# A hybrid encoder block on one core: the head of the u projection with joined loads, a second load of the first token block, filler products on a constant, and gate stores issued by SyncE

## The chip, the cores and the metric

The kernel runs on one core of one Trainium2 chip. The metric is the device time of one execution in microseconds, taken as the median of several runs.

## The reference

All data are float32. The block is one layer of the following, on 1040 rows (16 meta rows and 1024 tokens) of 1024 channels.

```python
def _mixer(xn, w_in, b_forget, ...):
    proj = xn @ w_in                                    # 1024 -> q, k, v, f_logit, u, gates
    q, k, v, f_logit, u, gates = jnp.split(proj, SPLITS, axis=-1)
    y_a = _forgetting_attention(q, k, v, f_logit, b_forget) @ w_attn_out
    z = jax.nn.gelu(_s5(u, ...))                        # diagonal complex state space model
    zg = z @ w_glu
    y_s = zg[..., :D_MODEL] * jax.nn.sigmoid(zg[..., D_MODEL:])
    g = jax.nn.sigmoid(gates)
    return (g[..., :D_MODEL] * y_a + g[..., D_MODEL:] * y_s) @ w_o

def reference(x, meta_tokens, ...):
    h = jnp.concatenate([meta, x], axis=1)
    h = h + _mixer(_rmsnorm(h, norm_mix_g), ...)
    h = h + _conv_ffn(_rmsnorm(h, norm_ffn_g), ...)     # causal depthwise conv, width 3
    return _rmsnorm(h, norm_final_g)[:, N_META:]
```

Here `u` is 512 channels wide, `gates` 2048, and `_s5` sends `u` in 32 groups of 16 channels through 64 complex states each.

## The kernel before, in words

**Products.** Every matrix product is a sum of three matmuls. An operand is split into a rounded part (`xhi`, `uh`, `whi`) and the remainder (`xlo`, `ul`, `wlo`), and hi·hi, lo·hi and hi·lo are added up in PSUM. The rounding is a cast on ACT, the remainder a subtraction on DVE or, for gate weights, an accumulating DMA (L144).

**The head.** The first product is `u`, the projection that feeds the state space model. The tokens lie transposed (channels on partitions, 8 chunks of 128, `KD = 8`) in four blocks of 272, 256, 256 and 256 tokens (`UBLK`). Block 0 is worked on while it is still being loaded: `FIRST` lists how many of the eight chunks come with each pair of loads, one load of `xa` (tokens) and one of `uraw` (the rows of the weight of u). For each chunk `features` makes `xhi` (ACT, L383) and `xlo` (DVE, L384), the weight is cast to `uh` (ACT, L409) and `ul` (DVE, L137), and `part` issues the products for the four groups of 128 channels of u (PE, L351 to L353) into four PSUM banks held open over all chunks. The loads are issued by SyncE (SP) in a fixed order through `load` (L313). They go on with blocks 1 to 3 (`xT`) and the tokens again with tokens on partitions (`xt`, `xm`), from which the root mean squares are taken.

**The normed features.** The u products use the tokens times the gain `g1T` alone, since the factor 1/rms of a token can be applied to the product. The gate and attention products need it in their input. So, once block 3 has been multiplied, `factors(b)` and `normed_features(b)` build the factors, multiply the raw blocks that are still in SBUF by them and split the result anew into `xhi` and `xlo`, block after block.

**Stores of u.** The u product goes through `usb` to DRAM (`u_d`) in 32 stores, 16 issued by SP and 16 by POOL (L455), and comes back in another layout as `U` (L1910): the first two of these loads are issued by SP.

**Gates.** `gate_chunk` multiplies one chunk of 128 gate channels, in three pieces of 342 rows, takes the sigmoid on ACT (L505) and stores the piece to DRAM (`g_d`), the store being issued by POOL (L506). The very first chunk has tiles of its own, `g0s`. All later pieces share two buffers of `gs`, so a sigmoid writes into a buffer whose store before last must have landed. The weights of each chunk are loaded by POOL (`raw`, L148) and cast by ACT (`whi`, L154).

**State space model.** Between the gate products the steps of the state space model run. For one quarter of the groups: DVE makes `Vm`, PE transposes it (L1903), ACT copies the result to `Wi` (L1904), PE multiplies `U` by `Wi` (L1916), ACT copies the products to `wr` and `wi` (L1919 and L1920), DVE does the recurrence on them (L1639 and two scans), and the same for the next quarter. `Tm` is loaded from `Kt` by SP (L1889).

**Order.** A scheduler settles the order of the instructions on each engine when the program is built. Each engine works through its list in that order, and one that waits holds up all that stands behind it.

Of the kernel before, what the change touches and what calls it, by code (L numbers as in the profile page):

```python
# [9 lines left out]
F = mybir.dt.float32  # L10
# [9 lines left out]
P = 128  # L20
D = 1024
KD = D // P
META = 16
# [5 lines left out]
SW = 512  # L29
# [14 lines left out]
UBLK = [(0, 272), (272, 256), (528, 256), (784, 256)]  # L44
UN = UBLK[0][1]
# [10 lines left out]


@with_exitstack
def block_kernel(ctx, tc, x, meta, xbt, x0t, g1t, w_q, w_k, w_v, w_f, w_u, w_g, b_f, w_ao, lam_d, bw_d, cw_d,
                 d_sk, l_dt, w_glu, w_o, g2, w_up, cwt_d, w_dn, gf, out, dbg=None, upto=99):  # L60
    nc = tc.nc
    dbg = dbg or {}
# [2 lines left out]
    V, S, GP, PE, SY = nc.vector, nc.scalar, nc.gpsimd, nc.tensor, nc.sync  # L65
# [7 lines left out]
    wp = pool(st_w, "wstream", bufs=2, side="right")  # L73
# [35 lines left out]
    g_d = dp.tile([2 * D, LQ], F, name="g_d")  # L109
# [26 lines left out]
    def split_lo(eng, out_, src, hi):  # L136
        return eng.tensor_tensor(out_, src, hi.bitcast(F), ALU.subtract)  # L137
# [151 lines left out]
    xhi = xp.tile([P, KD, L], R, name="xhi")  # L289
# [6 lines left out]
    st_n = ExitStack()  # L296
    n1 = pool(st_n, "norm1", side="left")

    uraw = [wp.tile([P, 2, SW], F, tag="raw", name="uraw") for _ in range(2)]
    uraw += [sp.tile([P, 2, SW], F, tag="Tm", name="uraw", bufs=2) for _ in range(2)]  # L300
    uh = [wp.tile([P, 2, SW], R, tag=tag, name="uh") for tag in ("whi", "wlo") for _ in range(2)]
    xm = sp.tile([META, D], F, tag="tq", name="xm", bufs=3)

    xT = {0: [sp.tile([P, 4, UN], F, tag="tq", name="xa", bufs=3) for _ in range(2)]}
    g1T = n1.tile([P, KD], F, name="g1T")
    ld = S.dma_start(g1T, g1t)
    after(S.activation(nhalf, one, AF.Copy, scale=-0.5), ld)
# [3 lines left out]
    def load(dst, src):  # L311

        queue.append(SY.dma_start(dst, src))  # L313
        if len(queue) > 1:
            after(*queue[:-3:-1])

    FIRST = [(0, 1), (1, 1), (2, 1), (3, 1), (4, 2), (6, 2)]
    for k, n in FIRST:
        load(xT[0][k // 4][:, k % 4:k % 4 + n], x0t[:, k:k + n])
        load(uraw[k // 2][:, k % 2:k % 2 + n], w_u[:, k:k + n])  # L320
    queue += ssm_loads()

    def load_block(b, tag):
        xT[b] = [sp.tile([P, 4, UBLK[b][1]], F, tag=tag, name="xT", bufs=2) for _ in range(2)]
        for h_ in range(2):
            load(xT[b][h_], xbt[b - 1, :, 4 * h_:4 * h_ + 4])

    place = {0: xm}

    def load_x(i):  # L330
        tag, bufs = ("Gm", 2) if i in (5, 6) else ("sy", 3)
        place[i] = (sp if i in (5, 6) else sio).tile([P, D], F, tag=tag, name="xt", bufs=bufs)
        load(place[i], x[P * (i - 1):P * i])

    load_block(1, "Wi")
    load(xm, meta)
    for i in range(5, 9):
        load_x(i)
    us2, ul2 = (sp.tile([P, 2, n, SW if n == 2 else NCH], dt, tag=tag, name=nm, bufs=1)
                for n, dt, tag, nm in ((CH, F, "pd", "usb"), (2, R, "pc", "ul")))  # L340
    ul = [sio.tile([P, 2, SW], R, tag="U", name="ul", bufs=2) for _ in range(2)] + [ul2[:, i] for i in range(2)]
# [7 lines left out]
    def part(ps, m, k, t, n):  # L349
        wh, wl = (w[k // 2][:, k % 2, P * m:P * m + P] for w in (uh, ul))  # L350
        PE.matmul(ps[:, :n], wh, xhi[:, k, t:t + n], start=(k == 0), stop=False)  # L351
        PE.matmul(ps[:, :n], wh, xlo[:, k, t:t + n], start=False, stop=False)
        PE.matmul(ps[:, :n], wl, xhi[:, k, t:t + n], start=False, stop=(k == KD - 1))  # L353
# [2 lines left out]
        return a.rearrange("p (n j) -> p j n", j=CH)  # L356

    head = []
    TB = [(0, 1, 2), (3, 4), (5, 6), (7, 8)]
    spread = {}  # L360
    rbs = sp.tile([P, 3, P], F, tag="dt8", name="rb", bufs=1)
    rs01 = sp.tile([P, UN + UBLK[1][1]], F, tag="wr", name="rsB", bufs=2)
# [16 lines left out]
    def features(b, k):  # L379

        t, n = UBLK[b]
        src, hi = xT[b][k // 4][:, k % 4], xhi[:, k, t:t + n]
        cp_ = S.activation(hi, src, AF.Copy, scale=g1T[:, k:k + 1])  # L383
        cut = V.scalar_tensor_tensor(out=xlo[:, k, t:t + n], in0=src, scalar=g1T[:, k:k + 1], in1=hi.bitcast(F),  # L384
                                     op0=ALU.mult, op1=ALU.subtract)
        return cp_, cut
# [15 lines left out]
        return us[m][:, :, t // CH:(t + n) // CH]  # L402

    first = [mm_ps() for _ in range(4)]
    for k0, n in FIRST:
        j, sl = k0 // 2, slice(k0 % 2, k0 % 2 + n)
        for k in range(k0, k0 + n):
            features(0, k)
        cp_ = S.copy(uh[j][:, sl], uraw[j][:, sl])  # L409
        split_lo(V, ul[j][:, sl], uraw[j][:, sl], uh[j][:, sl])  # L410
        for m in range(4):
            for k in range(k0, k0 + n):
                part(first[m], m, k, 0, UN)
    head.append(cp_)
    load_block(2, "Tm")
    load_block(3, "Gm")
    for i in range(1, 5):
        load_x(i)

    for m in range(4):  # L420
# [9 lines left out]
    for b in (2, 3):  # L430
        last = normed_features(b)[1]
        if b == 2:
            gate0 = [(sio if tag == "sy" else sp).tile([P, KD, P], dt, tag=tag, name="g0", bufs=n)
                     for dt, tag, n in ((F, "Tm", 2), (R, "sy", 3), (R, "Tm", 2))]
            GP.dma_start(gate0[0], w_g[KD])
            S.copy(gate0[1], gate0[0])
            lo_by_dma(gate0[2], gate0[1], w_g[KD])
        else:
            late.append(last)
        if b == 3:  # L440
            for q in (0, 1):
                factors(q)
            for q in (0, 1):
                cp_, last = normed_features(q)
            late.append(cp_)
        for m in range(4):
            ps = u_product(b, m)
            S.copy(us_part(b, m), by_chunks(ps[:, :UBLK[b][1]]))
# [41 lines left out]
    def gate_chunk(i, pl, tanh):  # L490
        whi, wlo = gate0[1:] if i == KD else wchunk(w_g[i], KD, GP, act=not tanh)
        if tanh:
            gs = pl.tile([P, LQ], F, tag="gs", name="gs", bufs=1)
        for t, n in QBLK[::-1] if i == KD else QBLK:
            ps = mm_ps()
            yield from dense_steps(ps[:, :n], whi, wlo, xhi[:, :, T0 + t:T0 + t + n],
                                   xlo[:, :, T0 + t:T0 + t + n], KD)
            if tanh:
                S.activation(gs[:, t:t + n], ps[:, :n], AF.Tanh, scale=0.5)
            else:  # L500
                if i == KD:
                    gs = g0s[:, t:t + n]
                else:
                    gs = pl.tile([P, LQ // 3], F, tag="gs", name="gs", bufs=2)
                S.activation(gs, ps[:, :n], AF.Sigmoid)  # L505
                GP.dma_start(g_d[P * i:P * i + P, t:t + n], gs)  # L506
        if tanh:
            GP.tensor_scalar(gs, gs, 0.5, 0.5, ALU.mult, ALU.add)
            if pl is not gp_ and i == KD - 1:
                okeep["g"] = gs  # L510
            else:
                SY.dma_start(g_d[P * i:P * i + P], gs)
# [1461 lines left out]
def _laid_out(x, meta_tokens, norm_mix_g, w_in, b_forget, w_attn_out, ssm_lambda_re, ssm_lambda_im, ssm_b_re, ssm_b_im,  # L1974
              ssm_c_re, ssm_c_im, ssm_d, ssm_log_dt, w_glu, w_o, norm_ffn_g, w_ffn_up, ffn_conv_w, ffn_conv_b,
              w_ffn_down, norm_final_g):
    import numpy as _np

    def by_rows(w):

        return w.reshape(-1, P, w.shape[1]).transpose(1, 0, 2)

    def blocks(w):

        return w.reshape(w.shape[0] // P, P, -1, P).transpose(2, 1, 0, 3)

    def twice(re, im):

        return _np.stack([_np.concatenate([re, im]), _np.concatenate([im, re])], axis=1)

    w = w_in[0]
    xT = by_rows(_np.concatenate([meta_tokens, x[0]]).T)
    q, k, v, f, u, g = _np.split(w, [AW, 2 * AW, 3 * AW, 3 * AW + H, 3 * AW + H + SW], axis=1)
    lam = _np.stack([ssm_lambda_re[0].T, ssm_lambda_im[0].T], axis=1)
    conv = _np.concatenate([ffn_conv_w[0], ffn_conv_b], axis=0)
    return dict(x=x[0], meta=meta_tokens, xbt=_np.stack([xT[:, :, t:t + n] for t, n in UBLK[1:]]),
                x0t=xT[:, :, :UN], g1t=norm_mix_g[0].reshape(KD, P).T, w_q=blocks(q), w_k=blocks(k), w_v=by_rows(v),
                w_f=by_rows(f), w_u=by_rows(u), w_g=blocks(g), b_f=b_forget[0], w_ao=blocks(w_attn_out[0]),
                lam=_np.concatenate([lam, lam]),
                bw=twice(ssm_b_re[0].transpose(1, 0, 2), ssm_b_im[0].transpose(1, 0, 2)),  # L2000
                cw=twice(ssm_c_re[0].transpose(2, 0, 1), ssm_c_im[0].transpose(2, 0, 1)),
                d_sk=ssm_d[0].reshape(G, GC).T, l_dt=ssm_log_dt[0], w_glu=blocks(w_glu[0]), w_o=w_o[0],
                g2=norm_ffn_g[0], w_up=blocks(w_ffn_up[0]), cwt=conv.reshape(4, -1, P).transpose(2, 0, 1),
                w_dn=w_ffn_down[0], gf=norm_final_g)
# [22 lines left out]
```

## Time and profile before

| | |
|---|---|
| median of 3 runs | 1443.2 us (1442.69 to 1445.39) |
| profiled execution | 1445.58 us |
| its span in the trace | 1443.8 us |
| TensorE (PE) busy | 1422.4 us, 99%, 9655 instructions |
| VectorE (DVE) busy | 1074.5 us, 74% |
| GpSimd (POOL) busy | 766.9 us, 53% |
| ScalarE (ACT) busy | 722.4 us, 50% |
| HBM traffic | 170.88 MB read, 71.71 MB written |

The profiled execution took 1.78 us more than the span of its trace, and 2.38 us more than the median of the runs. Instruction times below are microseconds from the start of the span. In a row of the timeline the two first numbers are start and duration, the bracket at the end is the idle time of the engine ahead of the row and what ended it. `SPq` and `POOLq` are DMA issues.

### The profile page before, as it was taken

How to read it: one execution, taken by the hardware profiler on the slowest of the kernel's cores; microseconds unless marked ns; L12 is line 12 of the kernel's file. 1: busy time of each engine (PE TensorE's matmuls, PEld its weight loads, DVE VectorE, ACT ScalarE, POOL GpSimd, SP SyncE). 2: the span in 40 equal slices, each digit the busy share in tenths (PEclk: the TensorE clock that was granted, in tenths of full speed). 3: DMA queues.
4: the chain of work that ended last, by engine and by line, in shares of the span. 5: the costliest groups of instructions: out<-in, count | busy, mean ns of one | idle time of the engine just before them, and what ended most of it. 6: DMA issues, size and time to landing. Idle time of an engine off the chain costs nothing. (4 is left out here: it accounts for less than half of the span.)

```text
span 1443.8 us, 26609 instructions
## 1 busy us (share of the span) xinstructions
PE 1422.4 (99%) x9655; PEld 1346.2 (93%) x9655; DVE 1074.5 (74%) x2203; ACT 722.4 (50%) x1419; POOL 766.9 (53%) x887
## 2 busy tenths in 40 slices
PE   8999999999999999999999999999999999999997
PEld 8999999988999999999879999999999999887886
DVE  7999788843657676656469987788877776788875
ACT  7646585423646565533646444444444445643433
POOL 2642258632456556415861335555555544887794
PEclk9999999999999999999999999999999999999999
DMA  8675644521147422167964156667753327964333
GB/s 297 177 180 164 156 108 148 154 96 30 38 139 162 123 63 71 41 230 245 261 154 138 63 132 173 170 166 186 190 139 112 99 79 253 330 203 145 111 87 117
DMA packets 92968, 214.06 MB, mean 148 GB/s; under 512 B 15090, under 2 KB 22898, under 8 KB 92452
## 3 DMA queue, kind: packets, MB, share of 16 engines
q1 hardware_dynamic: 73124, 166.32, 35.0%
q0 software_dynamic: 17696, 41.29, 15.0%
q10 hardware_dynamic: 2016, 4.74, 0.9%
q8 instruction: 76, 1.25, 0.4%
q14 instruction: 56, 0.46, 0.1%
HBM read 170.88 MB, written 71.71 MB: 168 GB/s over the span
## 5 line engine op out<-in xcount | busy, mean ns | idle before, releaser
L170 PE MATMUL mm<-xhi,whi 128*128 128x342 f32 (+2 forms) x480 | 156.9, 327 | 1.3 <-DVE q L137 1.0
L172 PE MATMUL mm<-xhi,wlo 128*128 128x342 f32 (+2 forms) x480 | 155.3, 324 | 0.0
L171 PE MATMUL mm<-xlo,whi 128*128 128x342 f32 (+2 forms) x480 | 155.2, 324 | 0.0
L1183 POOL TENSOR_TENSOR ov<-ov,og 128x1024 f32<-128x1024 f32 x21 | 50.8, 2419 | 118.2 <-ACT og L1182 115.9
L137 DVE TENSOR_TENSOR sw<-sf,sw 128x512 fp32r<-128x512 f32 x72 | 74.2, 1031 | 46.2 <-ACT sw L1174 45.2
L1174 ACT CAST sw<-sf 128x512 fp32r<-128x512 f32 x72 | 44.9, 623 | 109.0 <-POOL sf L1321 80.2
L170 PEld LDWEIGHTS mm<-xhi,whi 128*128 128x128 f32 x480 | 90.5, 188 | 2.7 <-PE sp L818 0.8
L172 PEld LDWEIGHTS mm<-xhi,wlo 128*128 128x128 f32 x480 | 90.3, 188 | 0.6 <-issue 0.2
L171 PEld LDWEIGHTS mm<-xlo,whi 128*128 128x128 f32 x480 | 90.4, 188 | 0.2
L867 ACT CAST th<-tp 128x256 fp32r<-128x256 f32 (+3 forms) x120 | 56.2, 472 | 61.5 <-PE tp L860 29.3
L137 DVE TENSOR_TENSOR tl<-tp,th 128x256 fp32r<-128x256 f32 (+3 forms) x120 | 65.1, 547 | 25.7 <-ACT th L867 24.2
L1321 POOL TENSOR_TENSOR sf<-raw,sf 128x512 f32<-128x512 f32 x36 | 62.5, 1736 | 38.6 <-DVE sw L137 38.5
L1321 POOL TENSOR_TENSOR sf<-raw 128x512 f32<-128x512 f32 x36 | 48.5, 1348 | 62.2 <-DVE sw L137 23.4
L234 PE MATMUL mm<-xhi,sw 128*128 128x258 f32 (+1 forms) x288 | 81.0, 281 | 0.0
L232 PE MATMUL mm<-xhi,sw 128*128 128x258 f32 (+1 forms) x288 | 80.8, 280 | 0.0
L233 PE MATMUL mm<-xlo,sw 128*128 128x258 f32 (+1 forms) x288 | 80.7, 280 | 0.0
L832 POOL TENSOR_SCALAR pt<-pt,nm 128x144 f32<-128x144 f32 (+4 forms) x72 | 52.5, 742 | 49.3 <-DVE nm L831 48.2
L1373 DVE SCALAR_TENSOR_TENSOR ov<-hv,cwt,ov 128x1024 f32<-128x1024 f32 x36 | 69.0, 1918 | 0.4 <-ACT ov L1371 0.4
L1174 ACT CAST sw<-raw 128x512 fp32r<-128x512 f32 x70 | 43.0, 620 | 47.7 <-PE sp L234 23.9
L830 ACT ACTIVATE pt<-pt,nm 128x144 f32<-128x144 f32 (+4 forms) x72 | 52.9, 736 | 26.8 <-DVE nm L829 26.4
L823 DVE CUSTOM_DVE_ANT_0 pt<-sp,fb 128x328 f32<-128x328 f32 (+8 forms) x112 | 46.4, 430 | 20.1 <-PE sp L818 11.3
L137 DVE TENSOR_TENSOR sw<-raw,sw 128x512 fp32r<-128x512 f32 x70 | 57.4, 823 | 4.9 <-ACT sw L1174 4.7
(722 smaller groups left out, 5726.9 us busy)
## 6 DMA issues: line engine op xcount, KB each, us to landing
raw<-in_w_up_dram SPq DMA_DIRECT2D x44, 512.0 KB, 3.7
t_d<-in_w_dn_dram POOLq DMA_DIRECT2D x44, 256.0 KB, 6.9
wr<-t_d SPq DMA_DIRECT2D x44, 256.0 KB, 3.7
ar<-a_d SPq DMA_DIRECT2D x41, 256.0 KB, 5.1
a_d<-ov SPq DMA_DIRECT2D x18, 512.0 KB, 2.6
wr<-in_w_dn_dram SPq DMA_DIRECT2D x33, 256.0 KB, 3.7
t_d<-in_w_dn_dram SPq DMA_DIRECT2D x22, 256.0 KB, 4.4
t_d<-t_d SPq DMA_DIRECT2D x22, 256.0 KB, 4.8
```

The costliest lines, as they stand in the source:

```text
L137: return eng.tensor_tensor(out_, src, hi.bitcast(F), ALU.subtract)
L170: yield PE.matmul(ps, whi[:, i, :], ahi[:, i], start=(i == 0), stop=False)
L171: yield PE.matmul(ps, whi[:, i, :], alo[:, i], start=False, stop=False)
L172: yield PE.matmul(ps, wlo[:, i, :], ahi[:, i], start=False, stop=(i == k - 1))
L232: PE.matmul(ps, a[0][:, i], bh, start=(i == 0 and not joins), stop=False, skip_group_check=True)
L233: PE.matmul(ps, a[0][:, i], bl, start=False, stop=False, skip_group_check=True)
L234: PE.matmul(ps, a[1][:, i], bh, start=False, stop=(i == kh - 1), skip_group_check=True)
L830: S.activation(pt[:n, :kc], pt[:n, :kc], AF.Exp, bias=nm[:n, 1:2], scale=0.125, accum_out=nm[:n, 2:3])
L867: S.copy(th[:kn, z:tw], tp[:kn, z:tw])
L1174: S.copy(hi, src)
L1321: sums.append(GP.tensor_tensor(f_, a, b, op))
L1373: V.scalar_tensor_tensor(out=o, in0=h_[:, j:SEQ + j], scalar=cwc(j, m), in1=o, op0=ALU.mult, op1=ALU.add)
```

## The change

1. The tokens of block 0 and the weight of u lie side by side in one input `xw` (784 columns per chunk), and eight loads bring them, one for each chunk, instead of twelve. For the first chunk the cast of the weight is done in two halves.
2. Thirteen products of a tile that DVE fills with 1.0 stand ahead of the first real product on PE. Their result, `busy`, is not used.
3. The order of the other loads changes, and block 0 is loaded a second time near the end of the list, since the buffers of `xw` have passed to others by the time its normed features are made.
4. Factors and normed features are made for block 1 first, then for block 0 (blocks 2 and 3 follow as before).
5. The stores of the gate chunk with tiles of its own and of the next two chunks (nine stores) are issued by SP instead of POOL.

```diff
-    uraw = [wp.tile([P, 2, SW], F, tag="raw", name="uraw") for _ in range(2)]
-    uraw += [sp.tile([P, 2, SW], F, tag="Tm", name="uraw", bufs=2) for _ in range(2)]
+    xw_s = [pl.tile([P, UN + SW], F, tag=tag, name="xw", bufs=n)
+            for pl, tag, n, c in ((wp, "raw", 2, 2), (sp, "Tm", 2, 2), (sp, "tq", 3, 3), (sp, "Gm", 2, 1)) for _ in range(c)]
     uh = [wp.tile([P, 2, SW], R, tag=tag, name="uh") for tag in ("whi", "wlo") for _ in range(2)]
+    V.memset(uh[3].bitcast(F)[:, 0, :UN], 1.0)
+    busy = t_ps("busy")
+    for _ in range(13):
+        PE.matmul(busy[:, :UN], uh[3][:, 0, :P], uh[3][:, 0, :UN], start=True, stop=True)
...
-    FIRST = [(0, 1), (1, 1), (2, 1), (3, 1), (4, 2), (6, 2)]
-    for k, n in FIRST:
-        load(xT[0][k // 4][:, k % 4:k % 4 + n], x0t[:, k:k + n])
-        load(uraw[k // 2][:, k % 2:k % 2 + n], w_u[:, k:k + n])
+    hold_block(1, "Wi")
+    for k in range(KD):
+        load(xw_s[k], xw[:, k])
+    for h_ in range(2):
+        load_half(1, h_)
     queue += ssm_loads()
...
-    for k0, n in FIRST:
-        j, sl = k0 // 2, slice(k0 % 2, k0 % 2 + n)
-        for k in range(k0, k0 + n):
-            features(0, k)
-        cp_ = S.copy(uh[j][:, sl], uraw[j][:, sl])
-        split_lo(V, ul[j][:, sl], uraw[j][:, sl], uh[j][:, sl])
+    for k in range(KD):
+        features(0, k)
+        for c in (slice(0, SW // 2), slice(SW // 2, SW)) if k == 0 else (slice(0, SW),):
+            cp_ = S.copy(uh[k // 2][:, k % 2, c], xw_s[k][:, UN:][:, c])
+        split_lo(V, ul[k // 2][:, k % 2], xw_s[k][:, UN:], uh[k // 2][:, k % 2])
...
+    load(xm, meta)
+    hold_block(0, "tq")
+    for i in (3, 4):
+        load_x(i)
+    for h_ in range(2):
+        load_half(0, h_)
+    for i in (1, 2):
         load_x(i)
...
-            for q in (0, 1):
+            for q in (1, 0):
                 factors(q)
-            for q in (0, 1):
+            for q in (1, 0):
                 cp_, last = normed_features(q)
...
-                GP.dma_start(g_d[P * i:P * i + P, t:t + n], gs)
+                (SY if i < KD + 3 else GP).dma_start(g_d[P * i:P * i + P, t:t + n], gs)
```

The start of PE's list before:

```order
L351 MATMUL mm<-xhi,uh 128x272
L352 MATMUL mm<-xlo,uh 128x272
L351 MATMUL mm<-xhi,uh 128x272
L352 MATMUL mm<-xlo,uh 128x272
L351 MATMUL mm<-xhi,uh 128x272
```

The start of PE's list after (`mm` and `po` are the four PSUM banks of u, line numbers are three higher than before):

```order
L305 MATMUL busy<-uh 128x272 x13
L354 MATMUL mm<-xhi,uh 128x272 x3
L354 MATMUL po<-xhi,uh 128x272
L355 MATMUL mm<-xlo,uh 128x272 x3
L355 MATMUL po<-xlo,uh 128x272
```

The thirteen products on the constant stand first, and of the first chunk all products on the rounded weight and rounded tokens now come ahead of those that need the remainder.

SP's list before, from the last loads of the head to the first load of `Tm`:

```order
L313 DMA xt<-in_x_dram 128x1024 x4
L1666 DMA sm_135<-in_cw_dram 128x1024
L1666 DMA bw<-in_bw_dram 128x1024
L1666 DMA sm_137<-in_d_sk_dram 16x32
L455 DMA u_d<-usb 16x8x130 x16
L1910 DMA U<-u_d 128x1040 x2
L1889 DMA Tm<-Kt 16x1024
```

The same part of SP's list after, with the stores of the gates (`g0s` the first chunk, `gs` the two buffers of later chunks):

```order
L317 DMA xT<-in_x0t_dram 128x1088 x2
L317 DMA xt<-in_x_dram 128x1024 x2
L1676 DMA sm_152<-in_cw_dram 128x1024
L1676 DMA bw<-in_bw_dram 128x1024
L1676 DMA sm_154<-in_d_sk_dram 16x32
L465 DMA u_d<-usb 16x8x130 x16
L1920 DMA U<-u_d 128x1040
L516 DMA g_d<-g0s 128x342 x3
L1920 DMA U<-u_d 128x1040
L516 DMA g_d<-gs 128x342 x6
L1899 DMA Tm<-Kt 16x1024
```

Nine gate stores now stand between the stores of u and the loads of `Tm`, three of them ahead of the second load of `U`, and the second load of block 0 (`x0t`) stands ahead of the last two token tiles.

ACT's list before, from the first sigmoids into the two `gs` buffers to the copies of the state space model's first quarter:

```order
L505 ACTIVATE gs<-po 128x342
L505 ACTIVATE gs<-mm 128x342
L154 CAST whi<-raw 128x1024
L143 ACTIVATE wlo<-whi 128x1024
L1904 COPY Wi<-sp 128x512
L1904 COPY Wi<-tp 128x512
L1919 COPY wr<-sp 64x260
L1920 COPY wi<-sp 64x260
L1919 COPY wr<-tp 64x260
...
L1920 COPY wi<-tp 64x260
L505 ACTIVATE gs<-mm 128x342
```

The same part of ACT's list after:

```order
L515 ACTIVATE gs<-po 128x342
L515 ACTIVATE gs<-mm 128x342
L154 CAST whi<-raw 128x1024
L143 ACTIVATE wlo<-whi 128x1024
L515 ACTIVATE gs<-mm 128x342 x2
L1914 COPY Wi<-sp 128x512
L1914 COPY Wi<-tp 128x512
L515 ACTIVATE gs<-po 128x342
L1929 COPY wr<-sp 64x260
L1930 COPY wi<-sp 64x260
```

The third and fourth sigmoid into `gs` have moved ahead of the copies of `Wi`, and the fifth between the copies of `Wi` and those of `wr` and `wi`; before, the third stood behind all of these copies. PE's list keeps its order in this stretch within a few places.

More of the change, by code (lines that the diff above doesn't have):

```diff
@@ L58, in block_kernel @@
 @with_exitstack
-def block_kernel(ctx, tc, x, meta, xbt, x0t, g1t, w_q, w_k, w_v, w_f, w_u, w_g, b_f, w_ao, lam_d, bw_d, cw_d,
+def block_kernel(ctx, tc, x, meta, xbt, x0t, xw, g1t, w_q, w_k, w_v, w_f, w_g, b_f, w_ao, lam_d, bw_d, cw_d,
                  d_sk, l_dt, w_glu, w_o, g2, w_up, cwt_d, w_dn, gf, out, dbg=None, upto=99):
@@ L297, in block_kernel @@
     n1 = pool(st_n, "norm1", side="left")
-    uraw = [wp.tile([P, 2, SW], F, tag="raw", name="uraw") for _ in range(2)]
-    uraw += [sp.tile([P, 2, SW], F, tag="Tm", name="uraw", bufs=2) for _ in range(2)]
+    xw_s = [pl.tile([P, UN + SW], F, tag=tag, name="xw", bufs=n)
+            for pl, tag, n, c in ((wp, "raw", 2, 2), (sp, "Tm", 2, 2), (sp, "tq", 3, 3), (sp, "Gm", 2, 1)) for _ in range(c)]
     uh = [wp.tile([P, 2, SW], R, tag=tag, name="uh") for tag in ("whi", "wlo") for _ in range(2)]
-    xm = sp.tile([META, D], F, tag="tq", name="xm", bufs=3)
-    xT = {0: [sp.tile([P, 4, UN], F, tag="tq", name="xa", bufs=3) for _ in range(2)]}
+    V.memset(uh[3].bitcast(F)[:, 0, :UN], 1.0)
+    busy = t_ps("busy")
+    for _ in range(13):
+        PE.matmul(busy[:, :UN], uh[3][:, 0, :P], uh[3][:, 0, :UN], start=True, stop=True)
+    xm = sio.tile([META, D], F, tag="sy", name="xm", bufs=3)
+    xT = {}
     g1T = n1.tile([P, KD], F, name="g1T")
@@ L315, in load, with hold_block, load_half @@
             after(*queue[:-3:-1])
-    FIRST = [(0, 1), (1, 1), (2, 1), (3, 1), (4, 2), (6, 2)]
-    for k, n in FIRST:
-        load(xT[0][k // 4][:, k % 4:k % 4 + n], x0t[:, k:k + n])
-        load(uraw[k // 2][:, k % 2:k % 2 + n], w_u[:, k:k + n])
+    def hold_block(b, tag):
+        xT[b] = [sp.tile([P, 4, UBLK[b][1]], F, tag=tag, name="xT", bufs=2 if b else 3) for _ in range(2)]
+    def load_half(b, h_):
+        load(xT[b][h_], xbt[b - 1, :, 4 * h_:4 * h_ + 4] if b else x0t[:, 4 * h_:4 * h_ + 4])
+    hold_block(1, "Wi")
[3 more added lines that the diff above has]
+        load_half(1, h_)
     queue += ssm_loads()
[L323 to L326, printed above, removed]
     place = {0: xm}
+    TB = [(0, 1, 2), (3, 4), (5, 6), (7, 8)]
     def load_x(i):
-        tag, bufs = ("Gm", 2) if i in (5, 6) else ("sy", 3)
-        place[i] = (sp if i in (5, 6) else sio).tile([P, D], F, tag=tag, name="xt", bufs=bufs)
+        pl, tag, bufs = (wp, "raw", 2) if i in (5, 6) else (sio, "sy", 3)
+        place[i] = pl.tile([P, D], F, tag=tag, name="xt", bufs=bufs)
         load(place[i], x[P * (i - 1):P * i])
[L335 to L338, printed above, removed]
     us2, ul2 = (sp.tile([P, 2, n, SW if n == 2 else NCH], dt, tag=tag, name=nm, bufs=1)
@@ L358, in block_kernel @@
     head = []
-    TB = [(0, 1, 2), (3, 4), (5, 6), (7, 8)]
     spread = {}
@@ L381, in features @@
         t, n = UBLK[b]
-        src, hi = xT[b][k // 4][:, k % 4], xhi[:, k, t:t + n]
+        src, hi = xT[b][k // 4][:, k % 4] if b in xT else xw_s[k][:, :UN], xhi[:, k, t:t + n]
         cp_ = S.activation(hi, src, AF.Copy, scale=g1T[:, k:k + 1])
@@ L404, in block_kernel @@
     first = [mm_ps() for _ in range(4)]
-    for k0, n in FIRST:
-        j, sl = k0 // 2, slice(k0 % 2, k0 % 2 + n)
-        for k in range(k0, k0 + n):
-            features(0, k)
-        cp_ = S.copy(uh[j][:, sl], uraw[j][:, sl])
-        split_lo(V, ul[j][:, sl], uraw[j][:, sl], uh[j][:, sl])
+    for k in range(KD):
[3 more added lines that the diff above has]
+        split_lo(V, ul[k // 2][:, k % 2], xw_s[k][:, UN:], uh[k // 2][:, k % 2])
         for m in range(4):
-            for k in range(k0, k0 + n):
-                part(first[m], m, k, 0, UN)
+            part(first[m], m, k, 0, UN)
     head.append(cp_)
-    load_block(2, "Tm")
-    load_block(3, "Gm")
-    for i in range(1, 5):
+    for b, tag in ((2, "Tm"), (3, "Gm")):
+        hold_block(b, tag)
+        for i in TB[b]:
+            load_x(i)
+        for h_ in range(2):
+            load_half(b, h_)
+    load(xm, meta)
+    hold_block(0, "tq")
+    for i in (3, 4):
+        load_x(i)
+    for h_ in range(2):
+        load_half(0, h_)
+    for i in (1, 2):
         load_x(i)
@@ L1996, in _laid_out @@
     return dict(x=x[0], meta=meta_tokens, xbt=_np.stack([xT[:, :, t:t + n] for t, n in UBLK[1:]]),
-                x0t=xT[:, :, :UN], g1t=norm_mix_g[0].reshape(KD, P).T, w_q=blocks(q), w_k=blocks(k), w_v=by_rows(v),
-                w_f=by_rows(f), w_u=by_rows(u), w_g=blocks(g), b_f=b_forget[0], w_ao=blocks(w_attn_out[0]),
+                x0t=xT[:, :, :UN], xw=_np.concatenate([xT[:, :, :UN], by_rows(u)], axis=2), g1t=norm_mix_g[0].reshape(KD, P).T, w_q=blocks(q), w_k=blocks(k), w_v=by_rows(v),
+                w_f=by_rows(f), w_g=blocks(g), b_f=b_forget[0], w_ao=blocks(w_attn_out[0]),
                 lam=_np.concatenate([lam, lam]),
```

## The prediction

> **What bounds the kernel now.** I read the page first, then PE's waits, then the timeline of each engine around the places that the change touches, and windows of the stretches between.
>
> ```profile
> span 1443.8 us, 26609 instructions
> PE 1422.4 (99%) x9655; PEld 1346.2 (93%) x9655; DVE 1074.5 (74%) x2203; ACT 722.4 (50%) x1419; POOL 766.9 (53%) x887
> ```
>
> TensorE is busy for 99% of the span. A change can only take time off by letting PE start sooner, by making its products faster, or by removing one of its waits, and it can only add time by stopping PE. PE's waits are few:
>
> ```profile
> PE mm L351 <- ACT uh L409: 5.1, 1, 5.1
> PE mm L1545 <- DVE hs L1555: 1.9, 1, 1.9
> ...
> PE sp L1916 <- DMA U<-u_d: 0.7, 1, 0.7
> ```
>
> (The columns are total us, times, longest us.) The largest wait is that at the very start, which parts 1 and 2 of the change are about. Here is how it comes about:
>
> ```profile
> 0.74 0.39 SPq L313 DMA_DIRECT2D xa<-in_x0t_dram  x1
> 1.19 0.42 SPq L313 DMA_DIRECT2D uraw<-in_w_u_dram  x1
> 3.06 0.52 ACT L383 ACTIVATE xhi<-xa,g1T 128x272 fp32r<-128x272 f32 x1 [0.39 <-DMA g1T<-in_g1t_dram]
> 4.41 0.62 ACT L409 CAST uh<-uraw 128x512 fp32r<-128x512 f32 x1 [0.83 <-DMA uraw<-in_w_u_dram]
> 5.08 0.60 PE L351 MATMUL mm<-xhi,uh 128*128 128x272 f32 x1 [5.08 <-ACT uh L409]
> ```
>
> The weight is asked for at 1.19, ACT gets it at 4.41, and the full cast of 0.62 us stands between it and the first product at 5.08. The windows tell how PE goes on (length, then busy us and instructions of PE, PEld, DVE, ACT, POOL, the granted clock, the DMA share and GB/s):
>
> ```profile
> 5.00:10.36 5.36, 5.28 (x23) 5.28 (x24) 3.95 (x7) 3.37 (x8) 0.00 (x0) 1.00 0.95 323
> 10.36:20.00 9.64, 9.64 (x79) 9.64 (x78) 7.73 (x17) 7.89 (x16) 0.00 (x0) 1.00 1.01 381
> 20.00:55.00 35.00, 35.00 (x297) 34.83 (x296) 33.05 (x139) 28.04 (x64) 20.81 (x29) 1.00 0.63 218
> 60.00:100.00 40.00, 40.00 (x267) 39.26 (x267) 38.30 (x80) 15.28 (x28) 21.25 (x41) 1.00 0.86 192
> 100.00:142.00 42.00, 41.35 (x304) 39.79 (x303) 41.27 (x72) 29.37 (x52) 10.35 (x18) 1.00 0.59 164
> ```
>
> Until 10.36 a product takes 5.28/23 = 0.230 us, after it 9.64/79 = 0.122 us, with the same tile sizes. PE ran slowly for the first 5.28 us of its work. The granted clock stands at 1.00 in both rows, so this column doesn't show it; the durations do. From 5.08 on PE is busy without a break to 100. So what the head gains is kept, unless something later stops PE.
>
> **The head, parts 1 and 2.** The joined load of the first chunk is 401 KB, issued where `xa` was, at 0.74. `xa` (139 KB) was used 2.3 us after its issue and the weight (256 KB) 3.2 us after its own, so the joined one lands between 3.06 and 3.96. I take 3.6, near the weight, since it is larger than either. Then ACT does half a cast (0.31 to 0.4) and `xhi` (0.52 by its row), and the first real product starts at about 4.5 instead of 5.08: 0.6 us gained, between 0.25 and 1.15.
>
> The thirteen products on the constant need only a fill by DVE and can start as soon as DVE's first rows do:
>
> ```profile
> 0.81 0.06 DVE L104 MEMSET one<- 128x1 f32 x1 [0.81 <-PEq L2014]
> ```
>
> With the fill at about 0.9 to 1.2 they run from 1.25 for 13 x 0.230 = 3.0 us, to 4.25, and end before the real ones can start; so they cost nothing as long as the joined load lands at 3.4 or later, and at most 0.3 us at its lower bound. What they move is the slow stretch. If PE again speeds up 5.28 us after its first product, that is at 6.5. From 4.5 to 6.5 the real products still run at 0.230, which loses 2.0 x (1 - 0.122/0.230) = 0.95 us. Before, the slow stretch lost 23 x (0.230 - 0.122) = 2.5 us. The gain is 1.5 us, between nothing (constants don't count as work, and the slow stretch starts at 4.5) and 2.5 (PE is fast by 4.5). Together the head gains **2.1 us**; I hold 1.35 to 2.85 for likely.
>
> [...]
>
> Does the head keep up? At 0.122 a chunk of twelve products takes 1.47 us, and its 401 KB take 1.05 us at the 381 GB/s of the window from 10.36. DVE and ACT do the same splits as before and are busy for 7.7 and 7.9 of 9.64 us there. So yes, narrowly. If they did not, each chunk would cost PE a few tenths, which the lower end of the gain holds.
>
> **The loads and the order of the normed features, parts 3 and 4.** The second load of block 0 brings 1.11 MB more, 2.9 us of transfer at 381 GB/s. The window from 20 to 55 has a DMA share of 0.63, so 13 of its 35 us are free. The normed features of blocks 0 and 1 are the same work in the other order. I cost both at nothing; the cover is that DMA slack, and without it 2.9 us of delay would come ahead of the normed features.
>
> **The gate stores, part 5, and what moved with them.** SP's issues cost SP time, not PE's, and nine issues taken off POOL help an engine that nobody on the path waits for. What matters is ACT. Its list now has two more sigmoids ahead of the copies of `Wi` and one more between those and the copies of `wr`. Each sigmoid writes a buffer whose earlier store must have landed. These are the rows of before:
>
> ```profile
> 80.54 1.11 POOL L506 DMA_DIRECT2D g_d<-gs  x2 [0.21 <-DMA u_d<-usb]
> 74.98 0.46 ACT L505 ACTIVATE gs<-po 128x342 f32<-128x342 f32 x1 [7.18 <-DMA u_d<-usb]
> 75.34 0.45 ACT L505 ACTIVATE gs<-mm 128x342 f32<-128x342 f32 x1
> 84.47 0.59 ACT L1904 COPY Wi<-tp 128x512 f32<-128x512 f32 x1
> 88.14 0.37 ACT L1919 COPY wr<-sp 64x260 f32<-64x260 f32 x1 [3.08 <-PE sp L1916]
> 91.26 0.46 ACT L505 ACTIVATE gs<-mm 128x342 f32<-128x342 f32 x1
> 87.49 0.61 PE L1916 MATMUL sp<-U,Wi 128*128 128x130 f32 x4
> 90.87 0.70 DVE L1639 TENSOR_TENSOR ta<-wr,pc 128x520 f32<-128x520 f32 x1 [0.72 <-ACT wr L1919]
> 98.49 1.21 DVE L1639 TENSOR_TENSOR Vm<-Vm,tv 128x1024 f32<-128x1024 f32 x1
> 99.84 0.63 PE L1903 MATMUL sp<-ident,Vm 128*128 128x128 f32 x4
> ```
>
> Before, the third sigmoid (91.26) came after all of this, and its buffer was long free. Now it stands ahead of `Wi`. How long a store of this line takes is in the answer for that line, and how loaded the DMA is in two windows:
>
> ```profile
> DMA to landing us min/median/max: 2.5/5.8/8.5
> 82.00:84.00 2.00, 2.00 (x16) 1.98 (x15) 2.00 (x8) 0.02 (x1) 0.55 (x1) 1.00 0.97 381
> 84.00:86.00 2.00, 2.00 (x16) 2.00 (x15) 2.00 (x8) 1.06 (x2) 0.00 (x0) 1.00 0.75 150
> ```
>
> I write the times on the clock of before; all of them shift with the head. SP's issue of the first `gs` store comes behind the stores of u, two `U` loads and three `g0s` stores. That is seven issues of some 0.5 to 0.96 us after 75.76, which is again about 80.5:
>
> ```profile
> 75.76 1.92 SPq L1910 DMA_DIRECT2D U<-u_d  x2
> ```
>
> It lands 5.8 us later (median) at 86.3, and the third sigmoid starts then, not at 76. The fourth follows, and the `Wi` copies end at about 88.3 instead of 85.06 (84.47 + 0.59), 0.8 us after PE wants them at 87.49. The fifth sigmoid waits for the store of the third: 86.3 + 0.46 and a landing of 3.8 us (between the minimum and the median, since the DMA is less loaded after 84), so it starts at 90.6 and the copies of `wr` 0.36 later, at about 91.0 instead of 88.14. Of these 2.8 us, 0.72 is idle time that DVE had ahead of `ta`, and 0.14 is the distance between the end of `Vm` (98.49 + 1.21) and PE's use of it at 99.84. DVE has no other slack: it is busy 41.27 of the 42 us after 100. So PE is stopped for 2.8 - 0.86 = **2.0 us**. The bounds are nothing, when the two landings together take less than 7.5 us, and 5.4 us, with a first landing of 8.5 and a second of 4.6 (80.54 + 8.5 + 0.46 + 4.6 + 0.36 = 94.4, 6.3 late).
>
> **The sum.** 2.1 gained, 2.0 lost: the profiled execution would go from 1445.58 to about 1445.5, and the median, which lies 2.38 below it, from 1443.2 to **1443.1 us**. A measurement of this kernel can tell about 0.2%, 2.9 us, from no change.
>
> **The rivals.** *The gain stays.* The stores land soon enough for ACT, within 7.5 us for two, and PE is never stopped. For it: before, the u stores, the `U` loads and the gate stores crowd into 80 to 84, and a calmer order could end that. Against it: the median of 5.8 and the share of 0.97. The time is 1443.2 - 2.1 = 1441.1; with the wait for `U` (0.7) gone too, 1440.4, and with the upper gain of the head 1439.7. [...]
>
> *Slower: ACT is held by its own gate stores.* Both landings are at the long end, `Wi` and `wr` come 6 us late, and DVE's recurrence and with it PE stand still: 5.4 lost against 2.1, which gives 1446.5. It decides from two landings of 12.7 us together, where the loss passes 5.0. For it: the `g0s` stores and `U` loads are in the same queue just ahead, POOL, freed of stores, can issue its weight loads earlier into the same window, and the same pattern comes back at the second quarter. Against it: the DMA share falls after 84.
>
> *The products on a constant do not bring the speed.* Only 0.6 of the head's gain is left: 1443.2 - 0.6 + 2.0 = 1444.6.
>
> **How the numbers follow.** The forecast has a chance of 0.47, the gain that stays 0.23, the slower case 0.22, the lost clock 0.08. Of the second, 0.15 lies more than 2.9 us below (where the wait for `U` goes too or the head gives its upper value); of the slower case 0.20 lies above by as much. That leaves 0.65 within. The range goes from 1440.3, the second case with all but its best, to 1446.5, the slower case.
>
> **What would show it.** Right: the first real product near 4.5, fast products from about 6.5, a row of a sigmoid ahead of the `Wi` copies whose idle time ends with a `g_d` store, copies of `wr` some 2.8 us late against PE's position, and PE waits on L1914 copies or on `Vm` of some 2 us by 100. Wrong: no such ACT wait, or no PE wait behind it (the first rival); PE waits of over 5 us before 142 (the second); durations of 0.43 us for real products until about 9.8 (the third).

## The result, and the profile after

The changed kernel takes 1454.69 us in the median of 6 runs (1451.77 to 1459.12), the kernel before 1444.2 in the median of 6 (1442.69 to 1446.92). The ratio is 1.0068, with a 95% interval of 1.0054 to 1.0082: about 10 us slower, outside the forecast range of 1440.3 to 1446.5. The profiled execution took 1455.52 us with a span of 1453.7, so 9.9 us more span than before.

The page, and PE's waits (total us, times, longest us), of the changed kernel:

```profile
span 1453.7 us, 26638 instructions
PE 1428.5 (98%) x9668; PEld 1351.8 (93%) x9668; DVE 1078.0 (74%) x2206; ACT 722.3 (50%) x1422; POOL 760.2 (52%) x878
```

```profile
PE sp L1926 <- ACT Wi L1914: 6.8, 1, 6.8
...
PE sp L1926 <- DMA U<-u_d: 1.6, 1, 1.6
...
PE busy L305 <- DVE uh L302: 1.2, 1, 1.2
...
PE mm L354 <- ACT xhi L385: 0.5, 1, 0.5
```

The one new wait is the one that the prediction had described: PE stands 6.8 us for `Wi`. The timelines of SP, ACT and PE around it:

```profile
78.80 0.38 SPq L1920 DMA_DIRECT2D U<-u_d  x1
79.65 2.36 SPq L516 DMA_DIRECT2D g_d<-g0s  x3
82.37 0.32 SPq L1920 DMA_DIRECT2D U<-u_d  x1
82.79 22.47 SPq L516 DMA_DIRECT2D g_d<-gs  x6
...
92.74 0.80 ACT L515 ACTIVATE gs<-mm 128x342 f32<-128x342 f32 x2 [11.35 <-DMA g_d<-gs]
93.43 0.59 ACT L1914 COPY Wi<-sp 128x512 f32<-128x512 f32 x1
93.90 0.62 ACT L1914 COPY Wi<-tp 128x512 f32<-128x512 f32 x1
95.80 0.46 ACT L515 ACTIVATE gs<-po 128x342 f32<-128x342 f32 x1 [1.29 <-DMA g_d<-gs]
96.16 0.36 ACT L1929 COPY wr<-sp 64x260 f32<-64x260 f32 x1
...
94.08 1.23 PE L1926 MATMUL sp<-U,Wi 128*128 128x130 f32 x4 [6.81 <-ACT Wi L1914]
```

ACT waited 11.35 us for the landing of a `gs` store before it could do the third and fourth sigmoid, and only then made `Wi`. The first of these stores was issued at 82.79 and ACT was released at 92.74. The answer for the line of the stores gives 9.9 us as the longest landing:

```profile
DMA to landing us min/median/max: 2.5/4.9/9.9
```

The windows behind the stop (length, then busy us of PE, PEld, DVE, ACT and POOL, the granted clock, the DMA share, GB/s) show a second cost:

```profile
87.00:90.00 3.00, 0.26 (x2) 0.00 (x0) 2.27 (x8) 0.00 (x0) 0.00 (x0) 1.00 1.02 279
90.00:94.00 4.00, 0.00 (x0) 0.00 (x0) 0.00 (x0) 1.26 (x4) 0.00 (x0) 0.81 0.26 92
94.00:97.00 3.00, 2.92 (x13) 2.93 (x14) 0.00 (x0) 1.67 (x6) 0.00 (x0) 0.50 0.33 120
97.00:100.00 3.00, 3.00 (x15) 3.00 (x14) 1.12 (x2) 2.14 (x6) 0.00 (x0) 0.61 0.16 58
100.00:105.00 5.00, 5.00 (x37) 4.41 (x36) 5.00 (x8) 2.65 (x5) 0.14 (x1) 1.00 0.00 2
```

The granted clock had fallen to 0.50 while PE still stood (0.75 from 92 to 93, 0.50 from 93 to 94), and until about 99.2 a product of 342 columns took 0.49 us instead of the 0.32 before the stop. Five us of work at a clock of 0.50 make an estimated 2.5 us lost. Together with the stop (6.8) and a wait for `U` that grew from 0.7 to 1.6 this makes 10.2 us, where the spans differ by 9.9.

The head gave nothing. Its timeline after:

```profile
4.21 0.40 ACT L410 CAST uh<-xw 128x256 fp32r<-128x256 f32 x1 [1.54 <-DMA xw<-in_xw_dram]
4.52 0.52 ACT L385 ACTIVATE xhi<-xw,g1T 128x272 fp32r<-128x272 f32 x1
...
5.09 1.05 PE L354 MATMUL mm<-xhi,uh 128*128 128x272 f32 x3 [0.54 <-ACT xhi L385]
...
9.79 0.88 PE L356 MATMUL mm<-xhi,ul 128*128 128x272 f32 x3
10.47 0.34 PE L356 MATMUL po<-xhi,ul 128*128 128x272 f32 x1
10.65 0.54 PE L354 MATMUL mm<-xhi,uh 128*128 128x272 f32 x3
```

The first real product starts at 5.09 (before: 5.08), and products are fast (0.29 us for one, 0.54 for three) only from 10.65 on (before: from 10.42). The thirteen products ended and left 0.54 us idle ahead of the first real one. The last u product starts at 55.17 (before: 54.84).

### The profile page after: what moved, and what is told of

It reads as the page before. It is cut to its first block, busy times and chain, and to the rows that moved or that the text cites. A ratio compares the mean times of both kernels' runs of the same rounds, so it can differ in the third digit from the quotient of the medians.

```text
span 1453.7 us, 26638 instructions
## 1 busy us (share of the span) xinstructions
PE 1428.5 (98%) x9668; PEld 1351.8 (93%) x9668; DVE 1078.0 (74%) x2206; ACT 722.3 (50%) x1422; POOL 760.2 (52%) x878
## 5 line engine op out<-in xcount | busy, mean ns | idle before, releaser
L170 PE MATMUL mm<-xhi,whi 128*128 128x342 f32 (+2 forms) x480 | 157.0, 327 | 1.0 <-DVE q L137 1.0
L170 PEld LDWEIGHTS mm<-xhi,whi 128*128 128x128 f32 x480 | 90.8, 189 | 1.8 <-PE sp L828 0.8
L233 PE MATMUL mm<-xlo,sw 128*128 128x258 f32 (+1 forms) x288 | 80.7, 280 | 0.0
```

The lines of the kernel that those rows point to most:

```text
L170: yield PE.matmul(ps, whi[:, i, :], ahi[:, i], start=(i == 0), stop=False)
L233: PE.matmul(ps, a[0][:, i], bl, start=False, stop=False, skip_group_check=True)
```

## The experiments

Ratios are to the kernel before, run on the same chip in the same set, with 95% intervals.

**The gate stores back to GpSimd.**

```diff
-                (SY if i < KD + 3 else GP).dma_start(g_d[P * i:P * i + P, t:t + n], gs)
+                GP.dma_start(g_d[P * i:P * i + P, t:t + n], gs)
```

> The changed kernel with part 5 undone: all gate stores are issued by GpSimd again, and with that the sigmoids go back behind the copies of Wi and wr on ACT. Theory (the loss is ACT held by sigmoids that wait for gate stores): the wait of PE for Wi (6.8 us) is gone, no slow clock after 87, and the time is 1443 to 1445.5, about that of before, since the head gained nothing in the trace of after. Rival (the head's new load order delays the stores of u, which end 3 us later, and everything behind them): PE still waits for U or Wi by 2 to 5 us, 1446 to 1450.

Measured: 1445.52 us (1443.13 to 1446.95), ratio 1.0003 (0.9995 to 1.0012). The wait for `Wi` is gone, and with it the loss. In this kernel's profiled execution the head did gain. Its first rows of real products, the one wait of PE between 60 and 130 us, and the windows behind that wait:

```profile
4.96 0.83 PE L354 MATMUL mm<-xhi,uh 128*128 128x272 f32 x3 [0.41 <-ACT xhi L385]
5.62 0.29 PE L354 MATMUL po<-xhi,uh 128*128 128x272 f32 x1
```

```profile
PE mm L170 <- ACT gs L515: 1.9, 1, 1.9
```

```profile
91.00:93.00 2.00, 0.52 (x5) 0.22 (x3) 2.00 (x3) 2.00 (x4) 0.76 (x2) 1.00 0.30 43
93.00:96.00 3.00, 2.62 (x11) 2.59 (x12) 3.00 (x5) 0.66 (x2) 2.35 (x4) 0.69 0.84 184
96.00:100.00 4.00, 4.00 (x23) 3.98 (x22) 4.00 (x6) 0.00 (x0) 0.00 (x0) 0.81 0.93 222
```

Products are fast from 5.62, and PE runs 2 us ahead of before until 90 (its last u product starts at 52.80 instead of 54.84). There it gives this back: the scheduler has now put two sigmoids behind the copies of `Kt`, PE waits 1.9 us for a PSUM bank that they free, and its clock falls after that (0.69 from 93 to 96).

**The old head with the gate stores by SyncE.**

```diff
-                GP.dma_start(g_d[P * i:P * i + P, t:t + n], gs)
+                (SY if i < KD + 3 else GP).dma_start(g_d[P * i:P * i + P, t:t + n], gs)
```

> The kernel before with part 5 alone: the nine gate stores issued by SyncE, the head as it was. The scheduler again puts two sigmoids ahead of Wi and one ahead of wr. Theory: PE waits for Wi by 3 to 7 us and runs slowly for some us after it, 1448 to 1454. Rival (the late stores of u in the new head are what makes the wait): the stores land about 3 us sooner here, so the wait is below 3 us, the clock stays up, and the time is 1444 to 1446.5.

Measured: 1452.67 us (1452.25 to 1455.56), ratio 1.0058 (1.0046 to 1.0070). Part 5 alone costs nearly all of what the whole change costs. PE's waits:

```profile
PE sp L1916 <- ACT Wi L1904: 4.1, 1, 4.1
PE mm L170 <- DVE fg L544: 4.0, 2, 2.5
```

SP's issues of the `gs` stores and ACT's wait for their landing:

```profile
80.77 18.85 SPq L506 DMA_DIRECT2D g_d<-gs  x6
ACT gs L505 <- DMA g_d<-gs: 11.0, 2, 10.9
```

The first store is issued at 80.77, and ACT goes on at 89.67, 8.9 us later. The wait for `Wi` is shorter here than in the changed kernel, and the forget gate, which stands on DVE's list behind the recurrence, holds PE up for another 4.0 (before: 0.3).

**The changed kernel with the order on ACT kept.** The third to fifth sigmoid into `gs` are ordered behind the last copy of the first quarter's `wr` and `wi`; the stores stay with SyncE.

```diff
-                S.activation(gs, ps[:, :n], AF.Sigmoid)
+                sig = S.activation(gs, ps[:, :n], AF.Sigmoid)
+                if i > KD:
+                    n_gs[0] += 1
+                    if 2 < n_gs[0] < 6:
+                        after(sig, WR0[-1])
...
+                    if qt == 0:
+                        WR0.append(cp_)
```

> The changed kernel with the stores still issued by SyncE, but the third to fifth sigmoid into gs ordered behind the last copy of wr and wi of the first quarter, as they stood before. Theory (the order on ACT is the cause, not who issues): 1443 to 1445.5, no wait of PE for Wi. Rival (the stores on SP's list are the cause, by delaying the second load of U and the loads of Tm): 1447 or more, with PE waiting for U or Tm.

Measured: 1444.75 us (1442.81 to 1448.65), ratio 1.0002 (0.9993 to 1.0012), no wait for `Wi`. SP's issues of the `gs` stores and ACT's wait for their landing:

```profile
83.90 13.72 SPq L525 DMA_DIRECT2D g_d<-gs  x6
ACT gs L520 <- DMA g_d<-gs: 2.8, 2, 1.5
```

The stores land no sooner: the first is issued at 83.90, and ACT gets its buffer back at 92.43. But `Wi`, `wr` and `wi` are copied by then. With the same engine issuing the same stores, the loss is gone. It is the order on ACT.

**Gate stores by GpSimd, without the thirteen products.**

```diff
-    V.memset(uh[3].bitcast(F)[:, 0, :UN], 1.0)
-    busy = t_ps("busy")
-    for _ in range(13):
-        PE.matmul(busy[:, :UN], uh[3][:, 0, :P], uh[3][:, 0, :UN], start=True, stop=True)
```

> As the first kernel of this set (gate stores by GpSimd), without the thirteen products on the constant. Theory (they move nothing, PE speeds up at about 10.4 us with or without them): within 1 us of the first kernel, fast products from 10.4. Rival (they do raise the speed earlier): 1 to 2 us slower than the first kernel.

Measured: 1448.56 us (1444.85 to 1453.49), ratio 1.0027 (1.0014 to 1.0040). This tells nothing of the products: without them the scheduler settled another order later on, and PE waits 4.4 us for the forget gate (`PE mm L170 <- DVE fg`). The next three experiments keep the order on ACT fixed.

**Seventeen products instead of thirteen,** on top of the kernel with the order on ACT kept:

```diff
-    for _ in range(13):
+    for _ in range(17):
```

> As e3_hold (gate stores by SyncE, third to fifth sigmoid held behind the copies of wr), with 17 products on the constant instead of 13, so that they reach to the first real product at about 5.1 and leave no gap of 1 us ahead of it. [...] Rival (products on a constant do not raise the speed): real products slow until 10.4, as e3_hold within 0.7 us.

Measured: 1443.26 us (1440.65 to 1445.19), ratio 0.9981 (0.9971 to 0.9991). It is faster than the kernel before, by 0.19%, and so than the changed one. The start of its timeline:

```profile
1.24 4.22 PE L308 MATMUL busy<-uh 128*128 128x272 f32 x17 [1.24 <-DVE uh L305]
5.40 0.73 PE L357 MATMUL mm<-xhi,uh 128*128 128x272 f32 x3
5.96 0.29 PE L357 MATMUL po<-xhi,uh 128*128 128x272 f32 x1
```

There is no idle time between the constant's products and the real ones (0.60 us with thirteen), and the real ones are fast from 5.96. They start 0.3 us later than with thirteen, and still PE is 1.9 us ahead of before at the end of the u products (the last starts at 52.94 instead of 54.84). Of this some 0.8 us is lost at 193, where PE waits 1.1 us for the forget gate (before: 0.3).

**The same with changing data.**

```diff
-    V.memset(uh[3].bitcast(F)[:, 0, :UN], 1.0)
+    V.memset(uh[3].bitcast(F)[:, 0, 0:UN:2], 1.37)
+    V.memset(uh[3].bitcast(F)[:, 0, 1:UN:2], -0.71)
```

> As e5_hold_17, but the tile that the 17 products use holds 1.37 and -0.71 in turn instead of one constant. Theory (only the gap matters): as e5_hold_17 within 0.7 us, fast by 8 us at the latest. Rival (data that doesn't change is no work that counts): fast by 8 us here and not in e5_hold_17, and 1 to 2.5 us faster than it.

Measured: 1444.46 us (1441.72 to 1447.38), ratio 0.9990 (0.9977 to 1.0002). Fast from 5.78, with the constant from 5.96. The medians lie 1.2 us apart, more than the expectation allowed, but the intervals overlap. The profiled execution waits 2.7 us for the forget gate instead of 1.1; it was the slowest of its twelve, so this doesn't tell what lies between the medians. For the speed of the first products the constant did as well as the changing data.

**None of these products,** with the order on ACT kept: the four lines taken out as above.

> As e3_hold without any product on the constant. Theory: first real product at about 5.1, fast products from 9.6 to 10.5, and a median that is the same as that of e3_hold or up to 1 us above it, 1444 to 1446. Rival (the 13 products help often): 1.5 us or more above e3_hold.

Measured: 1447.75 us (1445.45 to 1452.1), ratio 1.0009 (0.9997 to 1.0020), against 1.0002 (0.9993 to 1.0012) with thirteen. The intervals overlap, so whether thirteen help a little on average stays open. Against the seventeen products of the same set (0.9981) it is some 0.28% slower. In its profiled execution the speed came 3.5 us after the first product, at 8.6, sooner than expected.

**The kernel before with seventeen products and nothing else.**

```diff
+    V.memset(uh[3].bitcast(F)[:, 0, :UN], 1.0)
+    busy = t_ps("busy")
+    for _ in range(17):
+        PE.matmul(busy[:, :UN], uh[3][:, 0, :P], uh[3][:, 0, :UN], start=True, stop=True)
```

> The kernel before with 17 products on the constant ahead of its first real product, nothing else: loads, order of the blocks and issuers of the gate stores as before. Theory (the slow stretch at the start costs 2.5 us, and no other part of the change is needed for it): real products fast by 8 us at the latest, 1442 to 1443.5, 1 to 2.5 us below the kernel before. Rival: same as before within 0.7 us, slow until 10.4, or the gain is given back by a later wait of DVE or DMA.

Measured: 1445.24 us (1443.58 to 1447.35), ratio 1.0000 (0.9990 to 1.0010). The start of the old head came later here, and that was enough:

```profile
5.96 0.60 PE L355 MATMUL mm<-xhi,uh 128*128 128x272 f32 x1 [0.51 <-ACT uh L413]
...
10.18 0.29 PE L356 MATMUL po<-xlo,uh 128*128 128x272 f32 x1
```

Again half a microsecond of idle time stands ahead of the first real product, and again the speed comes only at 10.2 (before: 10.42). So seventeen products were not enough by themselves.

**Block 0 first again,** on the kernel with seventeen products:

```diff
-            for q in (1, 0):
+            for q in (0, 1):
                 factors(q)
-            for q in (1, 0):
+            for q in (0, 1):
```

> As e5_hold_17, but factors and normed features again for block 0 first (part 4 undone; block 0 is still loaded a second time). Theory (the order of the two blocks costs PE nothing by itself; it only moves when the stores of u start by 2 us or so): within 1 us of e5_hold_17. Rival (the reload lands late for block 0 first, so DVE stands waiting for xT): a wait of DVE or of PE between 30 and 60 us and 1.5 us or more above e5_hold_17.

Measured: 1456.42 us (1453.94 to 1459.11), ratio 1.0081 (1.0066 to 1.0096). The theory fell: against the same kernel with block 1 first the ratio goes from 0.9981 to 1.0081, some 14 us. PE's waits:

```profile
PE sp L1936 <- DMA U<-u_d: 2.8, 1, 2.8
PE mm L173 <- ACT xhi L388: 2.3, 1, 2.3
PE mm L175 <- DMA g<-in_w_g_dram: 1.9, 1, 1.9
...
PE mm L174 <- DVE xlo L389: 1.1, 1, 1.1
```

These make 8.1 us. Behind them PE ran slowly (granted clock 0.58 from 64 to 68 and 0.52 from 89 to 95, by these clocks an estimated 4.6 us lost), which covers the 11.1 us by which the spans of the two kernels differ. The rows of tokens that block 0's factors need are the last in the new list of loads; SP issued them from 31.27 to 40.8 (with block 1 first, from 31.56 to 33.2). With block 0 first, DVE's product of block 0 with its factors ran at 50.75 (before: 45.65) and all of block 1 stood behind it, while the first gate chunk takes its rows from the last to the first (`QBLK[::-1]`) and so wants block 1 ahead of block 0. It isn't the reload itself that was late, as the rival had it: DVE's waits name the factors (`rsB`, 2.1 us, of which 0.9 just ahead of block 1 at 59.60) and the squares that they are made from (1.3 us), not the tokens.

**Three `gs` buffers instead of two,** in the changed kernel:

```diff
-                    gs = pl.tile([P, LQ // 3], F, tag="gs", name="gs", bufs=2)
+                    gs = pl.tile([P, LQ // 3], F, tag="gs", name="gs", bufs=3)
```

> The changed kernel with three gs buffers instead of two, its order on ACT the same in the place in question. The third sigmoid then needs no landing, the fourth needs that of the first store, the fifth that of the second. Theory (ACT and with it Wi is released by the landing of the first store, at about 92): PE's wait for Wi stays at 5 to 7 us, since the fourth sigmoid also stands ahead of Wi; the second wait of ACT (1.3 us, ahead of wr) goes; 1451 to 1455. Rival (it is the second store that lands late, or the number of buffers alone): the wait for Wi falls below 3 us and the time to 1448 or less.

Measured: 1453.21 us (1452.49 to 1454.23), ratio 1.0059 (1.0046 to 1.0071). PE's wait and ACT's:

```profile
PE sp L1926 <- ACT Wi L1914: 6.5, 1, 6.5
```

```profile
ACT gs L515 <- DMA g_d<-gs: 12.5, 1, 12.5
```

One wait of ACT is left of two, and PE stands as long as before. So one more buffer didn't help (6.5 us instead of 6.8) with the fourth sigmoid, too, ahead of `Wi`.

**GpSimd's stores with seventeen products and the sigmoids behind `wr`:** the first edit above on the kernel with seventeen products.

> As e5_hold_17 with the gate stores issued by GpSimd. The scheduler puts the third and fourth sigmoid behind the copies of Kt here, as in e1_pool_stores. Theory (in e1_pool_stores PE waited 1.9 us for a sigmoid at 91 and ran slowly for some us after it, because its PSUM banks came free late; it is order on ACT again, not the issuer): that wait returns, and the time is 1 to 3 us above e5_hold_17. Rival (with GpSimd issuing, SP's list is shorter, U and Tm come sooner): the same as e5_hold_17 or below.

Measured: 1446.38 us (1444.67 to 1452.67), ratio 1.0014 (1.0000 to 1.0027). The wait for a PSUM bank at 92 returns (1.8 us, `PE mm L173 <- ACT gs`). With SyncE issuing, the scheduler sets the sigmoids just behind `wr`, with GpSimd behind `Kt`; the wait again is one of order. It explains 1.8 us of the 4.8 by which the ratio has risen against 0.9981; the profiled execution, near the fast end of the twelve, shows only 1.0 us more span. The rest stays open.

**The weights' transfers later.** GpSimd fills a tile thirteen times more and only then issues the small forget gate loads, `wlo` and `raw`, in the changed kernel:

```diff
-    GP.memset(wf.bitcast(F), 0.0)
+    for _ in range(14):
+        hold.append(GP.memset(wf.bitcast(F), 0.0))
...
+                after(ld, hold[-1])
```

> The changed kernel with PE's order and ACT's order around Wi kept, but GpSimd fills a tile fourteen times (some 7 us) before it issues the small forget gate loads and the two weight transfers of 512 KB that stood at 80.7 and 81.7. This takes 1 MB of transfers out of the time in which the first gs stores are under way. Theory (the first gs store took 10 us to land because the weight transfers share the DMA engines with it): it lands some 3 us sooner, PE's wait for Wi falls from 6.8 to 2.5 to 4.5 us, and the time to 1449 to 1452. Rival (the stores of u, the loads of U and the g0s stores fill the engines by themselves): the wait stays at 6 to 7 us and the time within 1 us of the changed kernel, 1453 to 1456.

Measured: 1453.1 us (1451.33 to 1454.31), ratio 1.0049 (1.0033 to 1.0065). ACT is released at 90.31 instead of 92.74, and PE's wait falls:

```profile
90.31 1.03 ACT L521 ACTIVATE gs<-mm 128x342 f32<-128x342 f32 x2 [9.56 <-DMA g_d<-gs]
...
PE sp L1932 <- ACT Wi L1920: 4.7, 2, 4.5
```

About 2.3 of the 6.8 us came from the 1 MB of weights that GpSimd, without stores to issue, asked for at 80.7 and 81.7: with these later the DMA share from 85 to 90 is 0.54 instead of 1.04. The wait (4.5 for the longer of the two) is at the upper end of what the theory gave; the time lies in the rival's range, in a set in which the kernel before stood at 1445.1. So the weights explain a third of the stop. What the rest comes from, no run shows.

## Why the prediction was wrong

- **What bounds the kernel, and where the danger lies:** right. PE was stopped where the prediction looked for it, by ACT, through sigmoids that wait for a gate store. Undoing the issuer or the order alone took the loss away.
- **The sum, and the forecast chosen among the rivals:** wrong. The sum had 2.1 gained and 2.0 lost. The changed kernel gained nothing and lost 10.2: 6.8 of standing for `Wi`, an estimated 2.5 of slow products behind it and 0.9 more for `U`. What happened is the slower rival, which had 0.22, and beyond its price of 5.4.
- **The first landing** was the term mis-sized most. The prediction took an issue at 80.5 and 5.8 us, so 86.3; it was 82.79 and about 9.9, so 92.7. The landing weighs more than the issue: with part 5 alone the issue was at 80.77, near the forecast, and the landing still took 8.9 us. (The prediction's seven issues ahead of that store are five by its own list; at 0.96 us each they give the same 80.5.) Two things were missed. SP's stores of u ended 3 us later; they began 2 us later, since DVE multiplied the u product by its factors at 62.58 instead of 60.52. Part 4 and the list of loads, which were costed at nothing, don't explain this alone: with both kept, that row stands at 60.34 with seventeen products and at 59.86 with none. What brings it stays open. And the weights' transfers came earlier into the same stretch (DMA share 1.04 from 85 to 90, and 0.54 with later weights), which the prediction named only as an argument for the rival; the runs price them at 2.3 us.
- **The price of a stop** was missing a term. 6.8 us of standing cost an estimated further 2.5, with the clock at 0.50 behind it. The prediction counted slow products at the start only.
- **The stop's place** was a little off. The prediction put the loss on DVE's recurrence (2.8 less 0.86 of slack) and had `Wi` late by only 0.8; `Wi` itself was 6.8 late, and PE waits there.
- **The head's gain of 2.1** was 0 in the changed kernel. The joined load was used at 4.21, not 3.6, though its bound of 3.96 was nearer. The larger failure is the slow stretch: the prediction held it for harmless that the thirteen products end before the real ones begin, and put the speed 5.28 us after the first of them, at 6.5; it came at 10.65. In the five kernels with a gap of 0.51 to 0.61 us it came at 9.4 to 10.8. With no gap and seventeen products it came at 5.96 and the head gained 1.9 us, near the 2.1: the filler products could bring the speed sooner, and that it didn't come with such a gap was not seen. The rival of products on a constant not bringing the speed (0.08) came true, for another reason than its own: with seventeen the constant brought it by 5.96, changing data by 5.78.
- **The issuer** by itself cost nothing that can be measured: with SyncE issuing and the order on ACT kept the ratio is 1.0002 (0.9993 to 1.0012), with GpSimd issuing 1.0003 (0.9995 to 1.0012).

## What to carry to other kernels

When an edit touches who issues a store, look where the scheduler then puts the instructions that reuse the stored buffer: here ACT, with its list in a fixed order, stood 11.35 us for one landing, and PE 6.8 us for what ACT had behind it. The landing to reckon with was the longest of its kind, not the median (9.9 and 4.9 us). The stop of 6.8 us cost PE its length and an estimated 2.5 us of slow products after it. With products that are to raise PE's speed, look for a gap ahead of the real ones: with 0.51 to 0.61 us of it the real ones here were fast only at 9.4 to 10.8, with 0.41 or none by 5.6 to 7.1.

## What was not expected of the hardware

- One profiled execution of each kernel shows this. Idle time of 0.5 us or more between filler products and real ones: the changed kernel (0.54), the kernel before with seventeen (0.51), the first kernel with the order kept (0.60), the one with three buffers (0.54) and the one with later weights (0.61) were slow until 9.4 to 10.8, as kernels without such products are (8.6 to 10.7). With 0.41 (the stores by GpSimd) and none (the four kernels with seventeen that had no gap) products were fast by 5.6 to 7.1. Whether the length of the gap decides or its place in time was not told apart.
- A stop of 1.85 us at about 92 lowered the clock in one kernel (0.69 and 0.81 in the windows behind it) and not in another (1.00 in the same windows of the kernel with GpSimd's stores and seventeen products). Five longer stops did: 2.5 us with part 5 alone (0.54 from 206 to 209), 2.7 with changing data (0.65 from 198 to 201), 2.8 with block 0 first (0.52 from 89 to 95), 4.5 with later weights (0.77 from 90 to 95) and 6.8 in the changed kernel (0.50 from 94 to 97).
- In the first 10 us of the changed kernel the granted clock stands at 1.00 while products of 272 columns take 0.43 us (0.29 later); after the stop at 90 it shows 0.50 with products of 342 columns at 0.49 us (0.32 otherwise). Here the column tells the second, not the first.
